# Splitting half of the feature weights on VectorE, and moving five smaller steps, in a hybrid decoder layer

## The chip, the core and the metric

The kernel runs on one core of a Trainium2 chip. The core has a matrix engine (TensorE, PE in the profile), three engines for element work (VectorE or DVE, ScalarE or ACT, GpSimd or POOL), a sync engine (SyncE or SP) that starts most transfers, and DMA engines that carry them. Each engine works through its own queue in order, and waits where an operand isn't there yet. The metric is the device time of one execution, in microseconds (us).

## What is computed

One decoder layer on 512 tokens of width 1024, everything in float32:

```python
proj = x @ w_in                                   # split into the ten inputs below
ret  = retention_chunkwise(rope(rq), rope(rk), rv)           # 4 heads x 128, chunks of 128
ret  = silu(rg) * (group_norm(ret) * ret_gn_gain)
sel  = indexer_topk(rope(iq), rope(ik), iw, topk=128)        # 8 heads x 64: top 128 keys a query
att  = sparse_attention(rope(aq), rope(ak), av, sel)         # 4 heads x 128
x = layer_norm(ALPHA * x + concat([ret, att]) @ w_out)
gate, up = split(x @ w_gate_up)                              # hidden width 2816
return layer_norm(ALPHA * x + (silu(gate) * up) @ w_down)
```

## The kernel before, in words

**Products of three.** A float32 operand is split into a high and a low part, and a product is three matmuls: high by high, high by low, low by high (`mm3`, L93 to L96). `split` (L85) makes the parts. ScalarE casts the high part (L86). The low part is source minus high part, and there are two ways to it. Kind "V": one subtraction on VectorE (L91). Kind "Q": ScalarE copies the negated high part (L88), and a DMA that POOL issues adds the source to it on its way (L89).

**The stream of weights.** `stream` (L172) lists the weight tiles of the projections and of the output projection with the kind of each of a tile's two halves. `wf` are the eight tiles of feature weights: keys and queries of attention, keys and queries of retention, so sixteen halves, k = 0 to 15. `weight` (L280) hands out a half and prepares three halves ahead: it puts `split` into the queues. The high and low parts live in four buffers each (`wh`, `wl`), the raw weights in three.

**The order.** The program's order is written by hand, with Python generators. The main generator yields at places between matmuls; at each of these, side generators are moved on. `pace(it, r)` moves a side generator by r units of its own cost figures a yield. `slots(main, plan)` runs the functions that `plan` lists for a yield's number. What is emitted first stands first in its engine's queue; the engines run at their own speed from there.

**The stages.**
- 0 to 28 us: the indexer's projection.
- 28 to 133 us: `proj_feature`, sixteen halves of 24 matmuls (`pf`). After each, VectorE turns the result by the rotary tables (`rope`, L217 to L219) and POOL adds (L221). Beside it runs `side`: `index_rope` (indexer's keys and queries: VectorE, POOL and POOL's DMAs), `logits` (scores, for query blocks 1 to 3: narrow matmuls `lg`, ScalarE, VectorE's sums), `topk` (48 rounds on VectorE, 16 for each block, over 256, 384 and 512 columns: a MAX8 at L388 and a replacement at L389).
- 133 to 217 us: `proj_token` for attention values, retention values and the gate (`pt`). Beside it, the rest of `side` and the 27 steps of `retention` (L517): scores, keys, states, outputs, then for each of the four chunks the norm (`ret_norm`, with a power on POOL, L426), `ret_scale` on VectorE (L502), `ret_gate` on POOL (L507) and `ret_turn`, which transposes the result on TensorE (L514, `rz`). At the end `att_score(0)`.
- 217 to 286 us: `mix_part`, the output projection, with attention in its slots: `sc_(b)` moves `att_score(b)` on by a step (scores and their maxima; exponentials; scaling by the sums, L550), `tr_` transposes (`apt`, L559), `pv_` multiplies by the values, `gate_(n)` splits the first gate weights.
- 286 to 308 us: the first gate blocks (`g_first`), between them the last norm (`sum_(3)`, `norm_half`, L620 and L621) and `combine` (L883), which forms sums and differences of token blocks for a product with fewer matmuls. `turn_` transposes such a tile (`trs`, L636), `rest` makes its low part (L642).
- 308 to 520 us: `g_cycle`, once for each of 22 hidden blocks. Each has gate and up weights, from which VectorE forms differences (`g_sum`, L762); `g_conv` splits the pieces A to D of the next blocks (`gh2C` and `gl2C` are the high and low part of block 2's piece C).
- 520 to 654 us: the down projection, the final norm, the stores.

Of the kernel before, what the change touches and what calls it, by code (L numbers as in the profile page):

```python
# [17 lines left out]
D = 1024  # L18
# [35 lines left out]
def hybrid_layer_kernel(ctx: ExitStack, tc: tile.TileContext, xT, x, pos, w0, wf, wt, wo,  # L54
# [114 lines left out]
        yield  # L169


    stream = [(wf[c], "VV" if c == 0 else "QQ") for c in range(8)]  # L172
    stream += [(wt[g, i], "QQ") for g in (1, 2, 0) for i in range(2)]
    stream += [(wo[c], "VV") for _ in range(2) for c in range(4)]
    limit = [len(stream)]
# [138 lines left out]
    def proj_feature(c):  # L314
        for i in range(2):
            h, l = weight()
            acc = psd(f"pf{c}_{i}")

            def items(acc=acc, h=h, l=l):
                for kt in range(KT):  # L320
                    cs = slice(kt * P, kt * P + P)
                    yield lambda cs=cs, kt=kt: mm3(acc, h[:, cs], l[:, cs], xh[kt], xl[kt], kt == 0, kt == KT - 1)

            yield from dense(list(items()), lambda i=i, acc=acc: rope(feats[c // 2][:, 2 * (c % 2) + i], acc, CT, ST), 3)
# [69 lines left out]
    def chain(*its):  # L394
        for it in its:
            yield from it

    def pace(it, r, credit=0.0):
        while True:
            credit += r  # L400
            while credit > 0.0:
                c = next(it, 0.0)
                credit -= 1.0 if c is None else c
                if c == 0.0:
                    break
            yield

    def run(main, *sides):
        for _ in main:
            for s in sides:  # L410
                next(s, None)
# [105 lines left out]
    def retention():  # L517
        steps = (((ret_keys, 0),), ((ret_score, 0),), ((ret_keys, 1),), ((ret_state, 0),), ((ret_score, 1),), ((ret_out, 0, 0),),
                 ((ret_out, 0, 1),), ((ret_state, 1),), ((ret_keys, 2), (ret_scale, 0)), ((ret_score, 2),), ((ret_out, 1, 0),),
                 ((ret_out, 1, 1),), ((ret_state, 2),), ((ret_score, 3), (ret_scale, 1)), ((ret_out, 2, 0), (ret_gate, 0)),  # L520
                 ((ret_out, 2, 1),), ((ret_gate, 1),), ((ret_out, 3, 0), (ret_scale, 2)), ((ret_out, 3, 1),), ((ret_turn, 0), (ret_gate, 2)),
                 ((ret_scale, 3),), ((ret_turn, 1), (ret_gate, 3)), (), ((ret_turn, 2),), (), ((ret_turn, 3),), ())
        for step in steps:
            for f, *a in step:
                f(*a)
            yield
# [52 lines left out]
    lg = chain(*[logits(j) for j in range(1, NB)])  # L579
    tk = chain(*[topk(j) for j in range(1, NB)])  # L580
    side = chain(index_rope(), lg, tk)
    run(chain(*[proj_feature(c) for c in range(4)]), pace(side, 1.0, -1.0))
    run(chain(*[proj_feature(c) for c in range(4, 8)]), pace(side, 1.0))
    run(proj_token(1), pace(side, 1.5))
    rt["decay"] = big.tile([P, 2, HEADS * P], F32, tag="s7", name="decay")
    dma(rt["decay"], decay_d)
    mixt[0] = unit("s8", "mrh", F32R), unit("s10", "mrl", F32R)
    rets = retention()
    run(proj_token(2), pace(side, 1.6), pace(rets, 1.2))
    tail = chain(rets, att_score(0))  # L590
    run(proj_token(0), pace(side, 1.2), pace(tail, 1.4))
    drain(tail)


# [85 lines left out]
    def slots(main, plan, *sides):  # L680
        for n, _ in enumerate(main):
            for f in plan.get(n, ()):
                f()
            for s in sides:
                next(s, None)

    def tr_(b, h):
        return lambda: att_tr(b, h)

    def pv_(b, h):  # L690
        return lambda: att_pv(b, h)
# [3 lines left out]
    def sc_(b):  # L695
        return lambda: next(sc[b])

    sums = {}

    def sum_(b):  # L700
        def f():
            sums[b] = norm_sum(x1[b], accm[b])
        return f
# [15 lines left out]
    def gate_(n):  # L719
        def f():  # L720
            hl = big.tile([P, 2, 1024], F32R, tag=("s6", "s7", "s9", "s1")[n], name=f"gb{n}")
            split(V, hl[:, 0], hl[:, 1], gates[n // 2][:, n % 2])
            gw[n, "B"] = hl[:, 0], hl[:, 1]
        return f
# [4 lines left out]
                           6: [sc_(1), pv_(0, 2)], 7: [pv_(0, 3)], 9: [tr_(1, 0)], 10: [tr_(1, 1)], 11: [tr_(1, 2), pv_(1, 0)],  # L729
                           12: [tr_(1, 3), pv_(1, 1)], 13: [pv_(1, 2)], 14: [pv_(1, 3), sc_(2)], 15: [gate_(0)]}, pace(side, 0.6))  # L730
    drain(side)
    slots(mix_part(0, 1), {0: [sc_(2)], 1: [gate_(1)], 2: [sc_(3)], 3: [sc_(2)], 5: [tr_(2, 0)], 6: [tr_(2, 1), sc_(3)], 7: [tr_(2, 2), pv_(2, 0)],
                           8: [tr_(2, 3), pv_(2, 1), sc_(3)], 9: [pv_(2, 2)], 10: [pv_(2, 3), gate_(2)], 11: [sum_(0)], 12: [tr_(3, 0), gate_(3)],
                           13: [tr_(3, 1)], 14: [tr_(3, 2), pv_(3, 0)], 15: [sum_(1), tr_(3, 3), pv_(3, 1)]})
    slots(mix_part(1, 0), {0: [pv_(3, 2), end_(0)], 1: [pv_(3, 3), end_(1)], 9: [early_(0, 0)], 10: [early_(0, 1)],
# [79 lines left out]
    def g_cycle(n, between=None):  # L815
        nxt = n + 1 if FIRST <= n + 1 < NF else None
        g_mm(n, "a", "A", 0, "s2", False)
        if n:
            g_end(n - 1)
        if between:  # L820
            next(between)
        gp[n]["c"] = psu(f"gc{n}")[:, :Q]
        g_mm(n, "c", "A", 1, "s1", True)
        t = tmp(f"gt{n}")
        gp[n]["t2"], gp[n]["t7"] = t[:, :Q], t[:, Q:]
        A.copy(gp[n]["t2"], gp[n]["a"])
        if n:
            g_conv(n + 1, "A")
        if nxt:
            g_open(nxt)  # L830
            g_mm(nxt, "a", "B", 0, "11", True)
        g_mm(n, "a", "C", 0, "s3", False)
        if nxt:
            g_t1(nxt)
            g_mm(nxt, "b", "B", 1, "12", True)
        c = gp[n]["c"]
        if n == NF - 1:
            c = tmp("gc")[:, :Q]
            A.copy(c, gp[n]["c"])
            g_mm(n, "c", "D", 0, "s4", False)  # L840
        A.copy(gp[n]["t7"], gp[n]["a"])
        V.tensor_tensor(gp[n]["t7"], gp[n]["t7"], c, op=ALU.add)
        if between:
            next(between)
        if n == 0:
            g_conv(1, "A")
        if n + 2 >= FIRST:
            g_conv(n + 2, "B")
        g_mm(n, "a", "C", 1, "22", False)
        if nxt:  # L850
            g_u1(nxt)
        g_sum(n + 2)
        g_conv(n + 1, "C", V if n > 1 else None)
        if n == 0:
            for m in range(FIRST):
                g_silu1(m)
        if n < NF - 1:
            g_mm(n, "c", "D", 0, "s4", False)
        A.activation(gp[n]["h2"], gp[n]["a"], AF.Silu)
        g_conv(n + 1, "D", V if n > 1 else None)  # L860
        g_load(n + 4)

    g_load(0)
# [24 lines left out]
    def g_first(n, which):  # L888
        g_mm(n, "ab"[which], "B", which, ("11", "12")[which], True)
        if which == 0:  # L890
            g_t1(n)
# [5 lines left out]
    g_first(0, 1)  # L897
    g_open(1)
    g_first(1, 0)
    sum_(3)()  # L900
    combine(2, G, ("s1", "s4"))
    g_add1(0)
    turn_("s2", 2)
    for i in range(2):
        norm_half(x1[3], *sums[3], gb, i)
    combine(3, V, ("s3", "s2"))
    g_first(1, 1)
    g_add1(1)
    combine(3, V, ("s1",))
    rest("s2", 2)  # L910
    g_open(2)
    g_first(2, 0)
    g_first(2, 1)
    g_open(3)
    g_first(3, 0)
    turn_("s2", 3)
    g_add1(2)
    rest("s2", 3)
    g_sum(1, V, slice(0, 2))
    g_first(3, 1)  # L920
    for b in (2, 3):
        turn_("s1", b)
        rest("s1", b)
# [249 lines left out]
```

## Time and profile before

| | |
|---|---|
| device time, median of 3 runs | 651.93 us (650.21 to 652.14) |
| profiled execution | 656.79 us |
| its span, first to last instruction | 654.0 us |
| TensorE busy | 626.8 us (96%) |
| VectorE busy | 473.7 us (72%) |
| ScalarE busy | 295.3 us (45%) |
| POOL busy | 118.8 us (18%) |

How to read it: the engines overlap, so their busy times don't add up. Where one engine is busy for nearly the whole span, the time is its work plus its waits. A busy share is a mean over stages; what a stage is limited by is read from its own windows. The granted clock is the share of its full speed that the chip gave TensorE in a stretch; a matmul's busy time grows when it falls.

### The profile page before, as it was taken

What the parts mean: (1) busy time and instruction counts of PE and PEld (TensorE: products, weight loads), DVE (VectorE), ACT (ScalarE), POOL (GpSimd) and SP (SyncE); (2) the same over time, 40 slices, a digit from 0 to 9 for tenths busy, and PEclk for the clock granted to TensorE, in tenths of its full rate; (3) what the DMA queues carried; (4) which work ended last, traced back from release to release, by engine and by line L of the source; (5) the groups of instructions that cost most, each with busy time, mean ns of one, the idle gap of its engine ahead of it and who ended that gap; (6) DMA issues with size and microseconds to landing.
All of it is one profiled execution on the core that took longest, in us unless ns stands there. A gap on an engine that the chain in (4) does not pass through costs nothing.

```text
span 654.0 us, 9798 instructions
## 1 busy us (share of the span) xinstructions
PE 626.8 (96%) x3792; PEld 558.0 (85%) x3792; DVE 473.7 (72%) x883; ACT 295.3 (45%) x514; POOL 118.8 (18%) x128
## 2 busy tenths in 40 slices
PE   9998899999999999998799999999999999999993
PEld 7976788888887868888699999999999988888883
DVE  6668378997879567999659888898898864333265
ACT  5625355334334657444645555555555643311100
POOL 1559623421373000041300000000000000000012
PEclk9999799999999999999989999999999999999997
DMA  8877975788543851352741332322313362321012
GB/s 301 276 215 176 210 201 138 169 197 213 136 122 121 306 218 65 128 129 69 162 142 67 127 116 79 129 81 114 130 65 129 129 208 82 129 99 62 2 43 86
DMA packets 25438, 91.14 MB, mean 139 GB/s; under 512 B 3056, under 2 KB 4208, under 8 KB 19760
## 3 DMA queue, kind: packets, MB, share of 16 engines
q1 hardware_dynamic: 18592, 71.51, 31.9%
q0 software_dynamic: 6224, 18.09, 14.3%
q10 hardware_dynamic: 576, 0.92, 0.4%
q8 instruction: 29, 0.48, 0.3%
q14 instruction: 17, 0.14, 0.1%
HBM read 69.80 MB, written 2.10 MB: 110 GB/s over the span
## 4 chain that ended last, share of the span: by engine, by line
PE 47%; DVE 6%; issue 2%; DMA 1%; POOL 1%; ACT 1%; DVEq 0%; POOLq 0%
PE ga L787 17%; PE gc L787 9%; PE gb L787 4%; PE dl L95 3%; PE dl L96 3%; PE dl L94 3%; PE dr L96 3%; PE dr L95 3%; PE dr L94 3%; DMA gl2C<-gs 1%; DVE gs L762 1%; DVE wl L91 1%; POOL rs L426 1%; DVE parts L642 1%; DVE cs L883 1%
## 5 line engine op out<-in xcount | busy, mean ns | idle before, releaser
L426 POOL TENSOR_TENSOR rs<-ve,half 128x1 f32<-128x1 f32 (+1 forms) x12 | 15.0, 1254 | 392.5 <-DVE ve L425 392.5
L86 ACT CAST wh<-raw 128x1024 fp32r<-128x1024 f32 x44 | 46.1, 1050 | 53.6 <-issue 20.1
L91 DVE TENSOR_TENSOR dl<-draw,dh 128x1024 fp32r<-128x1024 f32 x22 | 26.9, 1223 | 59.1 <-ACT dh L86 59.1
L96 PE MATMUL pf<-xh,wl 128*128 128x512 f32 x128 | 51.4, 402 | 4.9 <-DMA wl<-raw 4.9
L86 ACT CAST dh<-draw 128x1024 fp32r<-128x1024 f32 x22 | 23.2, 1053 | 69.5 <-PE dl L96 38.6
L94 PE MATMUL pf<-xh,wh 128*128 128x512 f32 x128 | 51.0, 398 | 0.0
L95 PE MATMUL pf<-xl,wh 128*128 128x512 f32 x128 | 50.9, 398 | 0.0
L94 PE MATMUL pt<-wh,xh 128*128 128x512 f32 x96 | 39.1, 407 | 0.0
L96 PE MATMUL pt<-wh,xl 128*128 128x512 f32 x96 | 37.5, 391 | 0.0
L95 PE MATMUL pt<-wl,xh 128*128 128x512 f32 x96 | 37.4, 390 | 0.0
L89 POOL DMA_DIRECT2D wl<-raw x26 | 23.7, 926 | 70.6 <-ACT wl L88 65.4
L96 PEld LDWEIGHTS pf<-xh,wl 128*128 128x128 f32 x128 | 24.7, 193 | 11.4 <-DMA wl<-raw 6.2
L94 PE MATMUL dl<-dh,h 128*128 128x512 f32 x88 | 34.2, 389 | 0.0
L95 PE MATMUL dl<-dl,h 128*128 128x512 f32 x88 | 34.2, 389 | 0.0
L96 PE MATMUL dl<-dh,h 128*128 128x512 f32 x88 | 34.2, 389 | 0.0
L96 PE MATMUL dr<-dh,h 128*128 128x512 f32 (+1 forms) x88 | 33.4, 379 | 0.0
L95 PE MATMUL dr<-dl,h 128*128 128x512 f32 (+1 forms) x88 | 33.4, 379 | 0.0
L94 PE MATMUL dr<-dh,h 128*128 128x512 f32 (+1 forms) x88 | 33.4, 379 | 0.0
L762 DVE TENSOR_TENSOR gs<-graw,gs 128x512 f32<-128x512 f32 x44 | 30.3, 688 | 0.8
L762 DVE TENSOR_TENSOR gs<-graw 128x512 f32<-128x512 f32 x44 | 30.1, 684 | 0.0
L91 DVE TENSOR_TENSOR wl<-raw,wh 128x1024 fp32r<-128x1024 f32 x18 | 21.8, 1220 | 9.9 <-ACT wh L86 9.9
L95 PEld LDWEIGHTS pf<-xl,wh 128*128 128x128 f32 x128 | 24.7, 193 | 4.9
(960 smaller groups left out, 1948.8 us busy)
## 6 DMA issues: line engine op xcount, KB each, us to landing
graw<-in_wgu_dram SPq DMA_DIRECT2D x22, 1024.0 KB, 4.8
wl<-raw POOLq DMA_DIRECT2D x26, 512.0 KB, 5.8
draw<-in_wd_dram SPq DMA_DIRECT2D x22, 512.0 KB, 4.6
raw<-in_wf_dram SPq DMA_DIRECT2D x8, 1024.0 KB, 8.5
raw<-in_wo_dram SPq DMA_DIRECT2D x8, 1024.0 KB, 5.0
raw<-in_wt_dram SPq DMA_DIRECT2D x6, 1024.0 KB, 6.1
w0s<-in_w_dram SPq DMA_DIRECT2D x8, 320.0 KB, 5.0
x<-in_x_dram SPq DMA_DIRECT2D x4, 512.0 KB, 5.0
```

Source lines behind the costliest of these rows:

```text
L86: A.copy(hi, src)
L89: nc.gpsimd.dma_start(lo.bitcast(F32), src, accum_op=ALU.add)
L91: eng_lo.tensor_tensor(lo, src, hi.bitcast(F32), op=ALU.subtract)
L94: T.matmul(acc, lhsT=lh, rhs=rh, start=first, stop=False, **kw)
L95: T.matmul(acc, lhsT=lh, rhs=rl, start=False, stop=False, **kw)
L96: T.matmul(acc, lhsT=ll, rhs=rh, start=False, stop=last, **kw)
L426: G.tensor_tensor(r[:, :n], e[:, :n], half[:, :n], op=ALU.pow)
L642: V.tensor_tensor(lo, turned[q, b], hi.bitcast(F32), op=ALU.subtract)
L762: eng.tensor_tensor(t[dst], a, b, op=ALU.subtract)
L787: T.matmul(gp[n][acc], lhsT=a[:, i * S + k * P:i * S + k * P + P], rhs=parts[q][:, b, k], start=first and j == 0, stop=j == 11, skip_group ...
L883: engs.tensor_tensor(c[q], how[q][0], how[q][1], op=how[q][2])
```

## The change

Five edits, all to order and place; what is computed stays the same.

1. In `stream`, the even half of each of the feature tiles 1 to 7 becomes kind "V"; the odd halves stay "Q". Tile 0 was "VV" and stays so. The side work's paces change: lower in the feature chunks, higher in the token projections.
2. In `retention`'s steps, `ret_gate(2)` moves ahead of `ret_out(3, 1)`, whose last act is the last norm.
3. In the slots of `mix_part(0, 1)`, the third step of `att_score(2)` (its scaling) moves from slot 3 to slot 2, and block 3's scores and `gate_(1)` move behind it, to slot 3.
4. Among the first gate blocks, `combine(2, G, …)` on POOL moves ahead of `sum_(3)`; one half of the last norm, `combine(3, …)` and two `g_first` move.
5. In `g_cycle`, block 1's piece C is split right behind the first copy to `gt` (L826) of cycle 0, and pieces C and D of block 2 become kind "V" where they were "Q".

```diff
-    stream = [(wf[c], "VV" if c == 0 else "QQ") for c in range(8)]
+    stream = [(wf[c], "VV" if c == 0 else "VQ") for c in range(8)]
...
-                 ((ret_out, 2, 1),), ((ret_gate, 1),), ((ret_out, 3, 0), (ret_scale, 2)), ((ret_out, 3, 1),), ((ret_turn, 0), (ret_gate, 2)),
+                 ((ret_out, 2, 1),), ((ret_gate, 1),), ((ret_out, 3, 0), (ret_scale, 2)), ((ret_gate, 2), (ret_out, 3, 1)), ((ret_turn, 0),),
...
-    run(chain(*[proj_feature(c) for c in range(4)]), pace(side, 1.0, -1.0))
-    run(chain(*[proj_feature(c) for c in range(4, 8)]), pace(side, 1.0))
-    run(proj_token(1), pace(side, 1.5))
+    run(chain(*[proj_feature(c) for c in range(4)]), pace(side, 0.85, -1.0))
+    run(chain(*[proj_feature(c) for c in range(4, 8)]), pace(side, 0.85))
+    run(proj_token(1), pace(side, 1.7))
...
-    run(proj_token(2), pace(side, 1.6), pace(rets, 1.2))
+    run(proj_token(2), pace(side, 1.8), pace(rets, 1.2))
...
-    run(proj_token(0), pace(side, 1.2), pace(tail, 1.4))
+    run(proj_token(0), pace(side, 1.5), pace(tail, 1.4))
...
-    slots(mix_part(0, 1), {0: [sc_(2)], 1: [gate_(1)], 2: [sc_(3)], 3: [sc_(2)], 5: [tr_(2, 0)], 6: [tr_(2, 1), sc_(3)], 7: [tr_(2, 2), pv_(2, 0)],
+    slots(mix_part(0, 1), {0: [sc_(2)], 2: [sc_(2)], 3: [sc_(3), gate_(1)], 5: [tr_(2, 0)], 6: [tr_(2, 1), sc_(3)], 7: [tr_(2, 2), pv_(2, 0)],
...
         A.copy(gp[n]["t2"], gp[n]["a"])
         if n:
             g_conv(n + 1, "A")
+        else:
+            g_conv(1, "C", None)
...
-        g_conv(n + 1, "C", V if n > 1 else None)
+        if n:
+            g_conv(n + 1, "C")
...
-        g_conv(n + 1, "D", V if n > 1 else None)
+        g_conv(n + 1, "D", V if n else None)
...
+    combine(2, G, ("s1", "s4"))
     sum_(3)()
-    combine(2, G, ("s1", "s4"))
     g_add1(0)
     turn_("s2", 2)
-    for i in range(2):
-        norm_half(x1[3], *sums[3], gb, i)
-    combine(3, V, ("s3", "s2"))
+    norm_half(x1[3], *sums[3], gb, 0)
     g_first(1, 1)
     g_add1(1)
-    combine(3, V, ("s1",))
+    norm_half(x1[3], *sums[3], gb, 1)
+    combine(3, V, ("s3", "s2"))
     rest("s2", 2)
     g_open(2)
     g_first(2, 0)
     g_first(2, 1)
+    combine(3, V, ("s1",))
     g_open(3)
     g_first(3, 0)
+    g_first(3, 1)
     turn_("s2", 3)
     g_add1(2)
     rest("s2", 3)
     g_sum(1, V, slice(0, 2))
-    g_first(3, 1)
```

What this does to the queues, at three places. First POOL's queue early in the feature chunks, in before: `wl4` and `wl5` are the low parts of the fifth and sixth half (k = 4 and 5), `kk3` the indexer's keys, `akT`, `qs` and `ql` results of ropes.

```order
L244 DMA kk3_359<-kk3_359 32x512
L89 DMA wl4_439<-raw2_279 128x1024
L221 TENSOR_TENSOR akT_362<-rt1_447,rt2_448 128x512
L250 TENSOR_TENSOR qs_465<-rt1_459,rt2_460 128x384
L251 TENSOR_TENSOR ql_358<-qs_465,qa_356 128x384
L89 DMA wl5_485<-raw2_279 128x1024
```

The same place in after:

```order
L244 DMA kk3_359<-kk3_359 32x512
L221 TENSOR_TENSOR akT_362<-rt1_445,rt2_446 128x512
L250 TENSOR_TENSOR qs_472<-rt1_466,rt2_467 128x384
L251 TENSOR_TENSOR ql_358<-qs_472,qa_356 128x384
L89 DMA wl5_483<-raw2_279 128x1024
```

The DMA for `wl4` is gone (VectorE makes it, ahead of the first rope of a chunk's result); the one for `wl5` stands where it stood, one DMA fewer behind the keys.

Second, VectorE's queue at the end of retention, in before: L425 is the last norm's variance, L437 the low part of a turned chunk, L502 `ret_scale(3)`, L388 and L389 one round of top-k.

```order
L425 TENSOR_SCALAR ve_1795<-mv_1786 128x4
L437 TENSOR_TENSOR mrl_1393<-rz0_1799,mrh_1392 128x4x128
L91 TENSOR_TENSOR wl28_1811<-raw14_1469,wh28_1810 128x1024
L502 TENSOR_SCALAR rz_1820<-ri3_1762,mv_1786,rs_1796 128x128 x4
L388 MAX m8_1837<-score_367 128x8
L389 MATCH_REPLACE score_367<-m8_1837,score_367 128x512
L437 TENSOR_TENSOR mrl_1393<-rz1_1840,mrh_1392 128x4x128
```

And in after:

```order
L425 TENSOR_SCALAR ve_1781<-mv_1772 128x4
L437 TENSOR_TENSOR mrl_1371<-rz0_1785,mrh_1370 128x4x128
L91 TENSOR_TENSOR wl28_1795<-raw14_1449,wh28_1794 128x1024
L388 MAX m8_1804<-score_367 128x8
L389 MATCH_REPLACE score_367<-m8_1804,score_367 128x512
L502 TENSOR_SCALAR rz_1807<-ri3_1746,mv_1772,rs_1782 128x128 x4
L388 MAX m8_1824<-score_367 128x8
L389 MATCH_REPLACE score_367<-m8_1824,score_367 128x512
L437 TENSOR_TENSOR mrl_1371<-rz1_1827,mrh_1370 128x4x128
```

A round of top-k over 512 columns stands ahead of the last scaling, where none stood between the same rows.

Third, VectorE's queue in cycle 1 of the gate blocks, in before: `gs3` are differences for block 3, L811 to L813 the closing sums of block 0.

```order
L762 TENSOR_TENSOR gs3_2_2975<-graw3_2769 128x512
L762 TENSOR_TENSOR gs3_3_2976<-graw3_2769,gs3_1_2974 128x512
L811 TENSOR_TENSOR gt1_2939<-gt1_2939,gc1_2926 128x256
L812 TENSOR_TENSOR hu0_2583<-hu0_2583,gt1_2939 128x256
L813 TENSOR_TENSOR hu0_2583<-hu0_2583,gt1_2939 128x256
```

And in after:

```order
L762 TENSOR_TENSOR gs3_2_2968<-graw3_2762 128x512
L762 TENSOR_TENSOR gs3_3_2969<-graw3_2762,gs3_1_2967 128x512
L91 TENSOR_TENSOR gl2C_2975<-gs2_2_2874,gh2C_2974 128x512
L91 TENSOR_TENSOR gl2C_2975<-gs2_3_2875,gh2C_2974 128x512
L91 TENSOR_TENSOR gl2D_2994<-graw2_2564,gh2D_2993 128x512
L811 TENSOR_TENSOR gt1_2932<-gt1_2932,gc1_2919 128x256
L812 TENSOR_TENSOR hu0_2576<-hu0_2576,gt1_2932 128x256
L813 TENSOR_TENSOR hu0_2576<-hu0_2576,gt1_2932 128x256
```

Three subtractions (the two halves of `gl2C`, and `gl2D`) now stand between the differences and the closing sums; the ScalarE copies and POOL DMAs that made them before are gone.

## Rows read from the trace of the kernel before

**Rows 1.** page, totals: busy us (share of the span), number of instructions.

```profile
PE 626.8 (96%) x3792; PEld 558.0 (85%) x3792; DVE 473.7 (72%) x883; ACT 295.3 (45%) x514; POOL 118.8 (18%) x128
```

**Rows 2.** waits of PE: instruction <- releaser: us in total, times, longest.

```profile
PE pf L96 <- DMA wl<-raw: 4.9, 3, 2.7
...
PE ga L787 <- DMA gl2C<-gs: 3.6, 1, 3.6
...
PE trs L636 <- DVE cs L883: 1.5, 1, 1.5
...
PE apt L559 <- DVE ast L550: 1.4, 1, 1.4
...
PE rz L514 <- POOL rzz L507: 1.1, 1, 1.1
```

**Rows 3.** windows: us, PE PEld DVE ACT POOL busy, PEclk, DMA share, GB/s.

```profile
50.00:60.00 10.00, 8.95 (x40) 7.04 (x39) 9.76 (x16) 5.56 (x8) 9.54 (x12) 1.00 0.68 129
...
60.00:70.00 10.00, 7.27 (x28) 5.65 (x27) 3.53 (x6) 3.77 (x5) 9.84 (x14) 0.82 0.96 224
...
290.00:300.00 10.00, 8.49 (x73) 8.29 (x72) 9.71 (x16) 2.29 (x5) 3.78 (x3) 1.00 0.00 0
...
320.00:330.00 10.00, 6.29 (x41) 5.79 (x40) 2.84 (x6) 2.23 (x6) 1.49 (x2) 0.79 0.77 176
```

**Rows 4.** timeline of PE, feature chunks: start, us, instruction, xcount [idle <-releaser].

```profile
52.80 0.50 PE L96 MATMUL pf<-xh,wl 128*128 128x512 f32 x1 [1.05 <-DMA wl<-raw]
...
63.95 0.39 PE L95 MATMUL pf<-xl,wh 128*128 128x512 f32 x1
...
67.07 0.79 PE L96 MATMUL pf<-xh,wl 128*128 128x512 f32 x1 [2.73 <-DMA wl<-raw]
...
73.21 0.44 PE L94 MATMUL pf<-xh,wh 128*128 128x512 f32 x1
```

**Rows 5.** timeline of POOL, feature chunks: issues of accumulating DMAs.

```profile
47.93 0.96 POOL L89 DMA_DIRECT2D wl<-raw  x1
...
52.55 0.87 POOL L89 DMA_DIRECT2D wl<-raw  x1
...
61.23 0.90 POOL L89 DMA_DIRECT2D wl<-raw  x1
```

**Rows 6.** timeline of DVE, feature chunks: one operation, twice.

```profile
49.26 1.40 DVE L248 TENSOR_TENSOR qa<-rt,rt 128x384 fp32r<-128x384 f32 x1
...
56.79 0.56 DVE L248 TENSOR_TENSOR qa<-rt,rt 128x384 fp32r<-128x384 f32 x1
```

**Rows 7.** groups of DVE by shape: busy us, mean ns | idle before.

```profile
L91 DVE TENSOR_TENSOR wl<-raw,wh 128x1024 fp32r<-128x1024 f32 x18 | 21.8, 1220 | 9.9 <-ACT wh L86 9.9
...
L388 DVE MAX8 m<-score 128x8 f32<-128x384 f32 x16 | 9.0, 560 | 0.5
```

**Rows 8.** timeline of DVE, POOL and PE, from retention to the attention scores.

```profile
160.55 0.69 DVE L456 TENSOR_TENSOR rst<-rs,decay 128x512 f32<-128x512 f32 x1 [3.48 <-DMA decay<-in_decay_dram]
...
203.67 1.30 POOL L507 TENSOR_TENSOR rzz<-rz,grg 128x512 f32<-128x512 f32 x1 [0.33 <-DVE rz L502]
...
208.03 0.60 PE L514 MATMUL rz<-ident,rzz 128*128 128x128 f32 x4
...
216.45 1.89 PE L538 MATMUL as<-akT,aqT 128*128 128x256 f32 x8
```

**Rows 9.** timeline of PE, gate pieces C and D of blocks 1 and 2.

```profile
315.28 0.38 PE L787 MATMUL ga<-parts,gh1C 128*128 128x256 f32 x1 [0.90 <-ACT gt L826]
...
318.97 0.28 PE L787 MATMUL gc<-parts,gh1D 128*128 128x256 f32 x1
...
327.20 0.58 PE L787 MATMUL ga<-parts,gl2C 128*128 128x256 f32 x1 [3.63 <-DMA gl2C<-gs]
...
332.95 0.28 PE L787 MATMUL gc<-parts,gh2D 128*128 128x256 f32 x1
```

## The prediction

> **What bounds the kernel now.** I read the page's totals first: TensorE is busy 626.8 us of the span of 654.0, VectorE 473.7, ScalarE 295.3 [rows 1]. So only two things can change the end by much: TensorE's idle time, and stretches in which its matmuls run at the lower clock. Second, TensorE's waits by releaser [rows 2]: nearly all of it lies in five places, and the change touches each. Third, the windows [rows 3]: the granted clock is 0.82 in the stretch with the longest wait of the feature chunks and 0.79 in the one with the longest of all, and 1.00 in the one ahead of them. A wait there costs more than its own length, because matmuls behind it run at 1.2 instead of 2.4 GHz for a while. Fourth, the timelines, for when each late thing would have been due.
>
> **Feature chunks (the kinds in `stream`).** Sixteen halves, k = 0 to 15, of 24 matmuls; between waits they start every 0.228 us (52.80 to 63.95, 49 steps) [rows 4]. The waits fall on k = 2, 4 and 6, each on a low half that a POOL-queued accumulating DMA delivers: 4.9 us idle, the longest 2.7 [rows 2]. After that one, 13 chunk matmuls and two narrower ones for the indexer scores take 6.14 us, 67.07 to 73.21 [rows 4]; at the pitch above, 13 × 0.228 and some 0.2 for the narrow ones, they would take about 3.2, so 2.9 is lost beyond the idle time. The loss is 4.9 + 2.9 = 7.8.
>
> All three late halves are even ones, and VectorE now makes the low parts of the even ones. Seven subtractions of 1.22 [rows 7], 8.5 us, join VectorE's queue; seven DMA issues of about 0.9 [rows 5] leave POOL's, and seven negated copies ScalarE's. Even halves no longer wait for a DMA. The odd ones do, and POOL's queue decides. For k = 5 the issue was at 52.55, and one issue of 0.96 less stands ahead of it, so 51.6. From issue to use it was 47.93 to 52.80, 4.87, and 61.23 to 67.07, 5.84 [rows 4, 5]. With 4.87 the low part of k = 5 is there at 56.5. It is due 24 steps after 52.80, at 58.3, less the 2.2 us of the two waits that are gone: 56.1. That is 0.4 late. But VectorE's subtraction now falls between POOL's tensor operations. The same VectorE operation took 1.40 at 49.26 and 0.56 at 56.79 [rows 6]: beside a busy POOL an operation with two input streams is stretched, and I take it that POOL's are too. If one such meeting costs POOL 1.2, about one subtraction, the issue is at 52.8 and k = 5 is 1.6 late. I take this end, since POOL has no gap there: 9.54 of 10 us busy [rows 3]. For k = 7 the same chain, with 4.87 to 5.84 from issue to use, gives 0.2 to 1.1 late, 0.8 taken; from k = 8 on the old order had no wait. So 2.4 of the 7.8 stays: gain **5.4**, bounds 3 (k = 5 lowers the clock as the 2.73 did) and 7.8 (no wait).
>
> The Trainium skill (SBUF — State Buffer, "Who interferes with whom") says that a VectorE instruction with two SBUF inputs contends with a GpSimd instruction that reads SBUF. This rule speaks against moving these splits to VectorE: by it k = 5 is 1.6 late and the sum below 12.9; without it 0.4 and 14.1. The two rows of 1.40 and 0.56 agree with it.
>
> Nothing stands behind the copies that leave ScalarE: it is idle over half of the span. SyncE's loads keep their order and their three buffers.
>
> **Later top-k (the paces).** The side work's lower pace in the chunks (0.85 for 1.0) leaves VectorE room for the splits and puts top-k rounds into the token projections. By the order, 26 of 48 rounds instead of 31 stand ahead of retention's first keys, and all 48 still end ahead of attention block 0's scores, as before. So five rounds more stand between these points, each a MAX8 of 0.56 [rows 7], a replacement over the same 384 columns, taken as long, and a short load: about 1.2, 6.0 in all. VectorE's wait of 3.48 for the decay table [rows 8] takes up part; 2.5 stays, of which I take 1.7 at the last norm. One more round, 512 wide, now stands ahead of the last scaling: 1.46, an estimate, 0.56 × 512/384 twice.
>
> **Retention gate.** Gate 2 goes ahead of the last norm's power on POOL, which waits for VectorE. TensorE's wait of 1.1 for it [rows 2] goes: gain 1.3 with its slow restart. But gate 3 ended at 203.67 + 1.30 = 204.97 [rows 8]; plus 1.7 and 1.46 that is 208.1. Turn 3 started at 208.03 [rows 8], is now due at 206.7, and so waits 1.4. Attention block 1's scores (216.45) [rows 8] need PSUM tiles that block 0's reductions on VectorE free, and VectorE is up to the whole 6.0 late there; I count 1.5 lost over scores and transposes. Gate and later top-k together: 1.3 − 1.4 − 1.5, about **−1.5**, a loss. Bounds +1.3 (the slack swallows the rounds) and −4 (the scores wait 4.0 instead of 1.5).
>
> **Softmax scaling.** Block 2's scaling goes one slot earlier, ahead of block 3's scores and the gate split. TensorE's wait of 1.4 before the transposes [rows 2] goes; VectorE has the same pieces in another order, and the moved ones aren't needed until block 3's transposes nine slots on. Gain **1.4**, bounds 0 (the lag above reaches this far) and 1.4.
>
> **Block sums.** POOL's two sums go ahead of VectorE's `sum_(3)`, and a gate group fills the pause before block 3's turn. TensorE's wait of 1.5 [rows 2] goes there, but VectorE is full at this point, 9.71 of 10 us in 290 to 300 [rows 3], and the next block's matmuls still need the rests that it makes. What TensorE doesn't wait before, it mostly waits after. Gain **0.5**, bounds 0 and 1.5.
>
> **Gate C and D splits.** C(1)'s split starts earlier, so that ScalarE's queue is free for the next copy of `gt`: the 0.90 that TensorE waits at 315.28 [rows 9] goes, gain **0.9**. C(2)'s low parts no longer go through ScalarE, POOL and a DMA. They landed so late that TensorE was idle 3.63 at 327.20, and the group then took 5.75 (to 332.95), where C(1)'s took 3.69 (315.28 to 318.97) [rows 9]: a loss of 3.6 + 2.1 = 5.7. On VectorE the three low halves of C(2) and D(2) take some 0.7 each (half the columns of 1.22 [rows 7], with an estimated 0.1 for the start), and it was busy only 2.84 of 10 us in 320 to 330 [rows 3]. They follow C(2)'s casts and the next block's differences and end at about 320.7 by its queue; they are due at about 322.3, a margin of 1.6. Gain **5.7**, bounds 4 (the margin is gone) and 5.7.
>
> **The sum.** 5.4 − 1.5 + 1.4 + 0.5 + 0.9 + 5.7 = 12.4, and 0.5 for the smaller waits on the same copies: **12.9 us**. The profiled execution took 656.79 for its span of 654.0, 4.9 above the median of 651.93. The same cut puts its like at 643.9, its span at 641.1 and the median at **639.0**. The bounds together make +3.9 and +19.1.
>
> **Rivals.**
> A. The chunks' waits only change place: odd halves are late in place of even ones, and the clock falls with them. For it: POOL keeps the odd halves' DMAs and is full to 60, and one wait of 2.73 was enough for the clock. Against it: half as many DMAs. The 5.4 shrinks to 0, 7.5 is gained: **644.4**. That the change doesn't do what it says (even halves still late, now on their casts) comes out here as well.
> B. No lag: the later rounds are swallowed, k = 5 lands in time, every term is at its upper bound. For it: VectorE is busy only 3.53 of 10 us in 60 to 70 [rows 3]. Against it: the slack of 3.48 is less than the 6.0 that is added. 19.1 is gained: **632.8**.
> C. Slower: VectorE's in-order queue becomes the bound of the chunks. The subtractions stand behind ropes and score sums, and TensorE has a lead of three halves, 3 × 24 × 0.228 = 16 us. Once VectorE's lag exceeds that, k = 6 to 14, five halves, are late; at the cost of the worst so far, 2.7 + 2.9, that is 28, less the 7.8 of the old waits and the 7.5 of the other edits: 12.7 slower, **664.6**. For it: VectorE is 9.76 of 10 us busy in 50 to 60 [rows 3]. Against it: 3.53 in the next ten, room for what is added.
>
> **How the numbers follow.** The forecast has a chance of 0.70, A 0.15, B 0.09, C 0.04; 0.02 lies between A and C, within 0.3% of before, about what a measurement of this kernel can tell from no change. The forecast's own bounds are 635 to 644; the range goes on to B at 632 and past A, to 646. Faster by over 0.3%: 0.94 (forecast, A, B); within: 0.02; slower: 0.04.
>
> **What will show it.** Right: no wait on an even half, at most about 3 us on odd ones up to 75 us, no clock under 0.9 there; no wait on `gl2C`, and a clock of 1.00 around 325; none on block 2's `ast`; a new one of about 1.4 on retention's last turn, or at the scores behind it. Wrong: `pf` waits of 5 us or more with a low clock (A), waits on VectorE's `wl` in the chunks (C), or waits on VectorE of over 4 us between 205 and 250, by which the later rounds would cost more than I gave them.

## The result, and the profile after

The changed kernel takes 647.35 us (median of 6 runs, 646.18 to 648.33) against 652.03 for the kernel before, timed beside it: a ratio of 0.9932, interval 0.9913 to 0.9951. That is 4.7 us less by the medians, where 12.9 were forecast, and above 646, the upper end of the range. The profiled execution took 646.18, its span is 643.7; of before they were 656.79 and 654.0. The trace of after is the shortest of its six executions (spans 643.7 to 645.9, granted clock 0.994 in the trace and 0.987 to 0.990 in the others), so a median execution of after has more low clock than the trace shows. One execution of 2196 us, of the version with the last pace at 1.0, is left out of its median and its ratio.

The page's totals of after, in the columns of [rows 1]:

```profile
PE 623.4 (97%) x3792; PEld 555.0 (86%) x3792; DVE 485.2 (75%) x893; ACT 287.5 (45%) x504; POOL 110.6 (17%) x118
```

VectorE has 11.5 us more, ScalarE 7.8 and POOL 8.2 less, as the edits say; TensorE's is 3.4 shorter with the same number of matmuls: the granted clock over the span is 0.994, where it was 0.984. The waits of TensorE in after, in the form of [rows 2]:

```profile
PE as L538 <- DVE mrl L437: 4.2, 1, 4.2
...
PE lg L369 <- DVE score L375: 1.4, 1, 1.4
...
PE rz L514 <- POOL rzz L507: 0.7, 1, 0.7
...
PE ga L787 <- ACT gt L843: 0.9, 2, 0.5
...
PE pf L96 <- DMA wl<-raw: 0.2, 1, 0.2
```

All five waits of [rows 2] are gone or small: on the DMA of a low half 4.9 became 0.2, and those on `gl2C`, `cs` and `ast` don't appear. Two new ones have come, both on VectorE: 4.2 on attention block 0's scores (`as`), 1.4 on the indexer's scores (`lg`). The 0.9 on `gt` is not new: before waits as long on the same copy, there in L841. The windows of after, in the columns of [rows 3]:

```profile
60.00:70.00 10.00, 9.81 (x45) 7.80 (x44) 8.34 (x10) 5.69 (x9) 6.95 (x8) 1.00 0.57 131
...
200.00:210.00 10.00, 5.08 (x26) 3.87 (x25) 9.79 (x22) 1.63 (x2) 1.28 (x1) 0.95 0.30 108
...
210.00:220.00 10.00, 10.00 (x41) 8.16 (x41) 7.00 (x28) 5.90 (x14) 0.00 (x0) 0.88 0.49 187
...
320.00:330.00 10.00, 9.54 (x79) 9.34 (x78) 9.00 (x18) 5.56 (x12) 0.00 (x0) 1.00 0.32 115
```

The clock is at 1.00 in 60 to 70 (0.82 in [rows 3]) and in 320 to 330 (0.79). It is below it now from 200 to 220, around the new wait: 0.95 and 0.88.

This table gives TensorE's way through the program, from the start of the first matmul of one kind to the first of the next. Since the profiled execution of before was 4.8 us above its median, the same kernel was profiled once more (`before_again`, below), and both stand here.

| from, to | before | before again | after | after less before | after less before again | forecast |
|---|---|---|---|---|---|---|
| start to `pf` | 27.90 | 28.51 | 27.76 | −0.14 | −0.75 | 0 |
| `pf` to `pt` (chunks) | 104.71 | 100.78 | 99.54 | −5.2 | −1.2 | −5.4 |
| `pt` to `rz` (projections, retention) | 63.08 | 63.08 | 63.03 | 0.0 | 0.0 | 0 |
| `rz` to `mx` (turns, scores) | 22.30 | 22.60 | 27.83 | +5.5 | +5.2 | +1.5 |
| `mx` to `ga` (output projection) | 67.91 | 67.87 | 66.36 | −1.6 | −1.5 | −1.4 |
| `ga` to `gc` (first gate blocks) | 18.11 | 18.14 | 17.40 | −0.7 | −0.7 | −0.5 |
| `gc` to block 3's `gc` (C and D splits) | 31.80 | 30.03 | 24.60 | −7.2 | −5.4 | −6.6 |
| from there to the end | 318.14 | 318.13 | 317.19 | −1.0 | −0.9 | 0 |
| span | 653.95 | 649.14 | 643.71 | −10.2 | −5.4 | |

Against the trace that the prediction was made from, the chunks gave 5.2 of the 5.4 forecast, and the only row far off is that from the turns to `mx`. Against the second trace of the same kernel the chunks gave 1.2. The experiments settle both rows. The 0.9 in the last row lies behind TensorE's last matmul, in the final norm and the stores, which no edit touches: from block 3's `gc` to that matmul all three traces take 307.4. Its cause stays open.

The place of the new wait, in the timeline of VectorE, ScalarE and TensorE in after:

```profile
184.18 0.69 DVE L475 TENSOR_TENSOR rstate<-rstate,rkv 128x512 f32<-128x512 f32 x1 [3.30 <-POOL rstate L474]
...
202.86 0.59 ACT L436 CAST mrh<-rz 128x512 fp32r<-128x512 f32 x1 [3.96 <-PE rz L514]
...
204.04 1.14 PE L538 MATMUL as<-akT,aqT 128*128 128x128 f32 x6
...
205.69 0.69 DVE L388 MAX8 m<-score 128x8 f32<-128x512 f32 x1
...
207.20 0.69 DVE L388 MAX8 m<-score 128x8 f32<-128x512 f32 x1
...
208.60 0.68 DVE L437 TENSOR_TENSOR mrl<-rz,mrh 128x512 fp32r<-128x512 f32 x1
...
209.33 0.80 PE L538 MATMUL as<-akT,aqT 128*128 128x128 f32 x2 [4.15 <-DVE mrl L437]
```

Three of block 0's four heads had a free PSUM tile at 204.04. The fourth needs the tile that retention's last turn (`rz`) holds until VectorE has made its low part (L437). Its high part is there at 202.86 + 0.59 = 203.45, but the subtraction stands behind top-k rounds in VectorE's queue, starts at 208.60, and TensorE goes on at 209.33, 4.15 late. From 204.04 to the first `mx` at 218.16 it is 14.1 us; before took 8.1 for the same: 4.15 of idle time, the rest at the lower clock of the two windows.

The same place in before:

```profile
188.42 0.69 DVE L475 TENSOR_TENSOR rstate<-rstate,rkv 128x512 f32<-128x512 f32 x1 [3.29 <-POOL rstate L474]
...
209.86 1.28 PE L538 MATMUL as<-akT,aqT 128*128 128x128 f32 x8
...
209.92 0.68 DVE L437 TENSOR_TENSOR mrl<-rz,mrh 128x512 fp32r<-128x512 f32 x1
```

The lines of the two kernels also tell which of the later rounds count. L475, a sum in retention's states, is the last place where VectorE sits idle ahead of that subtraction, 3.29 us in before and 3.30 in after. From there to the subtraction VectorE's queue has 7 rounds and takes 21.5 us in before, 9 rounds and 24.4 us in after. So two of the later rounds, 2.9 us, are on the way; the others stand ahead of a gap that VectorE has in both kernels. Counted from the first `pt`, the subtraction starts 4.0 us later than in before: 2.9 by the two rounds, 1.1 because L475 comes later. TensorE reaches the scores 0.5 earlier.

### The profile page after: what moved, and what is told of

Same layout as the page of the kernel before. It is cut to its first block, busy times and chain, and to the rows that moved or that the text cites. A ratio compares the mean times of both kernels' runs of the same rounds, so it can differ in the third digit from the quotient of the medians.

```text
span 643.7 us, 9760 instructions
## 1 busy us (share of the span) xinstructions
PE 623.4 (97%) x3792; PEld 555.0 (86%) x3792; DVE 485.2 (75%) x893; ACT 287.5 (45%) x504; POOL 110.6 (17%) x118
## 4 chain that ended last, share of the span: by engine, by line
PE 53%; DVE 4%; POOL 0%; issue 0%; ACT 0%; DVEq 0%; POOLq 0%
PE ga L787 19%; PE gc L787 10%; PE gb L787 5%; PE dl L95 3%; PE dl L96 3%; PE dl L94 3%; PE dr L96 3%; PE dr L95 3%; PE dr L94 3%; DVE wl L91 1%; DVE part L642 0%; POOL rs L426 0%; PE mx L95 0%; DVE gs L762 0%; PE mx L96 0%
## 5 line engine op out<-in xcount | busy, mean ns | idle before, releaser
L96 PE MATMUL pf<-xh,wl 128*128 128x512 f32 x128 | 50.1, 391 | 0.3 <-DMA wl<-raw 0.2
L91 DVE TENSOR_TENSOR wl<-raw,wh 128x1024 fp32r<-128x1024 f32 x25 | 32.5, 1308 | 14.8 <-ACT wh L86 14.8
L94 PEld LDWEIGHTS pf<-xh,wh 128*128 128x128 f32 x128 | 24.0, 188 | 4.5
```

The source lines that it names most:

```text
L91: eng_lo.tensor_tensor(lo, src, hi.bitcast(F32), op=ALU.subtract)
L94: T.matmul(acc, lhsT=lh, rhs=rh, start=first, stop=False, **kw)
L96: T.matmul(acc, lhsT=ll, rhs=rh, start=False, stop=last, **kw)
```

## Experiments

Each time stands as a ratio to the kernel before, which ran on the same chip beside it.

**The kernel before, once more.** No edit.

> The kernel before, unchanged, profiled a second time. Its first profiled execution took 656.79 us, 4.8 above the median of its timed runs. Theory 1 (the waits of that trace are in every run, and the 4.8 lie around the span): the span is again about 654, with waits on the low halves of 4.9 us, on gl2C of 3.6, and windows at a granted clock of 0.8 after both. Theory 2 (that execution had one stretch at the low clock that most have not): a span of about 649 to 650, with one of the two stretches (60 to 80 us, or 320 to 340) at a clock near 1.0; its idle time is then still there, but shorter by the matmuls that run at half rate behind it.

Median 652.77, ratio 1.0003 (0.998 to 1.0027); span of the profiled execution 649.1. Its waits, and its windows:

```profile
PE pf L96 <- DMA wl<-raw: 4.1, 2, 3.0
...
PE ga L787 <- DMA gl2C<-gs: 2.8, 1, 2.8
```

```profile
60.00:70.00 10.00, 6.96 (x32) 5.45 (x31) 3.59 (x6) 3.58 (x6) 9.92 (x13) 1.00 0.95 222
...
70.00:80.00 10.00, 10.00 (x53) 8.61 (x52) 6.38 (x13) 4.59 (x10) 5.56 (x5) 1.00 0.98 235
...
320.00:330.00 10.00, 6.76 (x44) 6.26 (x43) 5.47 (x10) 3.45 (x8) 0.00 (x0) 0.83 0.81 204
```

The wait on the low halves is there, and the longest, 3.0, is longer than the 2.7 of [rows 2]. But the clock stays at 1.00 behind it, where the first trace had 0.82 in 60 to 70. So the 2.9 us of half-rate matmuls that I counted among the chunks' loss don't belong to every execution. The spans and granted clocks of 63 runs of before say how often it may have been so: from 648.3 at 0.990 to 654.4 at 0.984, median 650.7; nine of them have a granted clock as low as 0.984 or 0.985, and one alone is longer than the 653.95 of the execution that I read. Theory 2 holds. The low clock around `gl2C`, 0.83, is in both traces, if shorter here.

**The C and D splits alone.**

```diff
+        else:
+            g_conv(1, "C", None)
...
-        g_conv(n + 1, "C", V if n > 1 else None)
+        if n:
+            g_conv(n + 1, "C")
...
-        g_conv(n + 1, "D", V if n > 1 else None)
+        g_conv(n + 1, "D", V if n else None)
```

> The kernel before with the fifth edit alone (splits of gate pieces C and D). Theory 1: every run of before has the 3.6 us wait on gl2C and the low clock behind it, so this edit alone takes 6.6 to 7.2 us off the median, to about 645. Theory 2: the low clock there is not in every run, and 4 to 5 us come off. A rival, that the wait only moves to the next block's pieces: 0 to 2 us off.

Median 646.28, ratio 0.9909 (0.9878 to 0.9939): 5.9 us by the ratio, 6.5 by the medians. By the ratios this one edit brings more than the whole change does, though the two intervals overlap.

```profile
320.00:330.00 10.00, 9.54 (x79) 9.34 (x79) 8.62 (x16) 5.34 (x11) 0.00 (x0) 1.00 0.36 134
```

The clock is 1.00, and `gl2C` is not waited for. The forecast of 6.6 for this edit is right, within what the interval allows (4.0 to 8.0 us); the time lies between the two theories of the expectation.

**The even halves on VectorE alone, with the paces of before.**

```diff
-    stream = [(wf[c], "VV" if c == 0 else "QQ") for c in range(8)]
+    stream = [(wf[c], "VV" if c == 0 else "VQ") for c in range(8)]
```

> The kernel before with the even halves of the feature chunks split on VectorE and nothing else, the paces as before. Theory 1: the waits on the low halves and the low clock behind the third go, 5 us less, if the side work does not need the lower pace; without it, waits on VectorE of 1 to 3 us turn up in the chunks, and 3 to 4 come off. Theory 2: the low clock behind the third wait is not in every run of before, and 2 to 3 us come off the median. Retention and attention have the queue order of before, so no wait of several us at the scores.

Median 652.87, ratio 1.0001 (0.9983 to 1.0018): nothing gained, a miss of both theories.

```profile
PE lg L369 <- DVE score L375: 4.6, 1, 4.6
```

```profile
70.00:80.00 10.00, 7.56 (x25) 6.29 (x26) 8.43 (x14) 2.05 (x4) 4.52 (x4) 0.66 0.65 173
```

The chunks' waits on DMAs are gone and one of 4.6 has come: the indexer's score matmuls need a PSUM tile that VectorE empties (L375), and VectorE is behind its splits and ropes. The clock is 0.66 in the ten us around it. One of the added splits, in VectorE's and POOL's timeline, shows how VectorE falls behind:

```profile
65.04 1.61 POOL L221 TENSOR_TENSOR akT<-rt,rt 128x512 f32<-128x512 f32 x1
...
65.08 2.66 DVE L91 TENSOR_TENSOR wl<-raw,wh 128x1024 fp32r<-128x1024 f32 x1 [1.42 <-ACT wh L86]
```

Ahead of the split VectorE sat idle for 1.42, until ScalarE had cast the high part, with ropes and score sums standing behind the split in its queue. The split then took 2.66, where the group's mean in before was 1.22 [rows 7]; a POOL operation that reads two tiles started 0.04 ahead of it. This is rival C's mechanism, VectorE's queue as the bound of the chunks, at a smaller price than I gave it and at another place: the indexer's scores, not the halves.

**The first edit whole: halves and paces.** The edit above and the five changed paces.

> The kernel before with the first edit whole: halves on VectorE and the changed paces. If the later top-k rounds cost what the trace of after shows between the last retention turn and the output projection (6.0 us), this is slower than halves_alone by about 6 us, and about as long as before (within 2 us). If that wait comes from the moved retention gate instead, it is as fast as halves_alone or faster, and shows no wait of 4 us at the scores.

Median 653.88, ratio 1.0017 (0.9999 to 1.0035): no faster than before, and not told apart from it or from the halves alone. So the expectation held against before, and not against the halves alone, which had gained nothing either.

```profile
PE rz L514 <- POOL rzz L507: 3.6, 1, 3.6
...
PE as L538 <- DVE mrl L437: 1.4, 1, 1.4
...
PE lg L369 <- DVE score L375: 1.4, 1, 1.4
```

The lower pace does what it is for: 1.4 on `lg` instead of 4.6, and the stretch from `pf` to `pt` takes 99.5 us as in after, against 103.5 with the halves alone. But the rounds that it moved come back on retention: 3.6 on the last norm's gate, 1.4 at the scores. Here the retention gate stands where it stood, and the price, 22.30 grown to 27.65 from `rz` to `mx`, is that of after. So the moved gate is not what makes the price; it decides whether TensorE pays it on the gate or at the scores.

**After without the first edit.** Halves and paces as in before, edits 2 to 5 kept.

> After without the first edit: the sixteen halves and the paces as in before, the other four edits kept. Theory 1 (the first edit as a whole costs time, because VectorE falls behind): the chunks wait for DMAs as in before (4 us idle), the scores do not wait, and the time is that of the fifth edit alone, 646.3, less what edits 2 to 4 bring in the trace (about 1.1, 1.4 and 0.6): 643 to 644, faster than after by 3 to 4 us. Theory 2 (edits 2 to 4 bring nothing, the first edit is neutral): 646 to 647, the same as after.

Median 643.03, ratio 0.9868 (0.984 to 0.9896), against 0.9932 for after: faster by 0.0064, 4.2 us, and the intervals don't overlap. Theory 1 holds.

```profile
PE pf L96 <- DMA wl<-raw: 3.6, 2, 2.5
...
PE as L538 <- DVE mrl L437: 1.3, 1, 1.3
```

The chunks wait for DMAs as before (their clock is 1.00 here too), and the scores wait 1.3. Edits 2 to 4 are the difference from the C and D splits alone, 0.0041, 2.7 us, with intervals that overlap; their terms in the forecast were 1.3, 1.4 and 0.5. By the two traces edit 3 brings 1.6 (`mx` to `ga`), edit 4 0.7 (`ga` to `gc`), and edit 2 nothing: from `rz` to `mx` it is 22.3 against 22.4, with 1.3 idle at the scores in place of 1.2 on the gate.

**After with the old paces,** the halves kept.

> After with the paces of before, the halves on VectorE kept. Theory 1 (the lag comes with the later rounds): no wait over 1 us between the last turn and the output projection; but a wait of some 4.6 us of the indexer's score matmuls on VectorE in the chunks with the low clock behind it, as in the halves alone; in all 643 to 645. Theory 2 (the moved retention gate makes the wait of 4.2 at the scores): it is still there, and the time is 647 or more.

Median 645.58, ratio 0.9900 (0.9873 to 0.9927), 2.1 us faster than after by the ratio, with intervals that overlap.

```profile
PE lg L369 <- DVE score L375: 4.5, 1, 4.5
...
PE as L538 <- DVE mrl L437: 1.4, 1, 1.4
```

The wait at the scores shrinks from 4.2 to 1.4 and the one in the chunks grows from 1.4 to 4.5. The rounds add to VectorE's queue in one place or the other; the paces choose where TensorE meets it. The 1.4 is not the later rounds': it is there with the halves and the paces of before too, where edit 2 is kept (1.3, above).

**After with the last pace at 1.0.** Rounds of top-k move behind block 0's scores: four by the expectation, three by the trace, where 45 of 48 stand ahead of them.

```diff
-    run(proj_token(0), pace(side, 1.5), pace(tail, 1.4))
+    run(proj_token(0), pace(side, 1.0), pace(tail, 1.4))
```

> After with one number changed: the side work's pace in the last token projection is 1.0 instead of 1.5, so that four rounds of top-k move from ahead of attention block 0's scores to behind them. Theory 1 (VectorE's queue at the last turned chunk is the wait): the 4.2 us at the scores shrink by two to four rounds of 1.46 each, to under 2, the low clock behind them goes, and 3 to 6 us come off: 641.5 to 644.5. Rival (the rounds are work that VectorE has to do before the softmax of block 2 anyway, so the wait only moves there): the waits turn up before 245 us on the scores of block 1 or the transposes, and the time stays within 1.5 us of after.

Median 641.27, ratio 0.9839 (0.9808 to 0.9869): 6.1 us faster than after by the ratio.

```profile
PE as L538 <- DVE mrl L437: 1.5, 1, 1.5
...
PE rz L514 <- POOL rzz L507: 0.8, 1, 0.8
```

The wait at the scores is 1.5 instead of 4.2, the clock from 200 to 220 is 1.00, and no wait turns up at the transposes of block 2. The rounds were not needed there yet; they only stood in the way.

**After with 1.15 in the last four feature tiles.** The rounds go earlier, into a stretch in which VectorE had gaps.

```diff
-    run(chain(*[proj_feature(c) for c in range(4, 8)]), pace(side, 0.85))
+    run(chain(*[proj_feature(c) for c in range(4, 8)]), pace(side, 1.15))
```

> After with one number changed in the other direction: the pace in the last four feature tiles is 1.15 instead of 0.85, so that top-k rounds move into the stretch from 90 to 130 us, where VectorE was idle for 8 us of 40; all rounds but none of the splits then stand ahead of the last two turns. Theory 1: the wait at the scores goes (4.2 and about 1.8 of low clock), the chunks gain no wait of over 1 us: 641 to 643. Rival: the indexer's score matmuls then wait for VectorE in the chunks, as with the old paces (4.6 us), and the time is 645 or more.

Median 641.71, ratio 0.9845 (0.9817 to 0.9874): 5.7 us faster than after.

```profile
PE rz L514 <- POOL rzz L507: 1.1, 1, 1.1
...
PE lg L369 <- DVE score L375: 1.4, 1, 1.4
```

```profile
200.00:210.00 10.00, 8.86 (x46) 7.19 (x45) 8.07 (x22) 4.38 (x11) 1.29 (x1) 1.00 0.38 138
```

No wait on `as` is left; VectorE is busy 8.07 of 10 us from 200 to 210, against 9.79 in after. From L475 to the last turn's low part VectorE now has 5 rounds and takes 19.3 us; with the last pace at 1.0 it has 6 and takes 20.3. Moving the rounds later or earlier gives the same 6 us back: so much was the price of VectorE's queue at that one place.

**The moved retention gate, undone in two surroundings:** in after, and in the version above.

```diff
-                 ((ret_gate, 2), (ret_out, 3, 1)), ((ret_turn, 0),),
+                 ((ret_out, 3, 1),), ((ret_turn, 0), (ret_gate, 2)),
```

> After with the second edit undone: gate 2 of retention is again behind the last norm on POOL. Theory 1 (VectorE's lag is what TensorE waits for, wherever it waits): the wait only sits one place earlier, some 3 to 4 us on the third turn (rz) on POOL's rzz and 1 to 2 at the scores, and the time is that of after within 1 us, 646.5 to 648.5. Theory 2 (the moved gate is worth its 1.1 us beside the lag): 1 to 1.5 us slower than after, 648.5 or more.

> The version with the pace of 1.15 in the last four feature tiles (641.7), and in it the second edit undone. There VectorE is not late, so this prices the moved gate by itself: if it is worth what TensorE's wait in before was (1.1 idle, 1.3 with its restart), this is 1 to 1.5 us slower, 642.8 to 643.3; if the wait only moves to the next thing that comes late (the gate or norm of the last block), the two are the same within 0.5 us.

In after, undoing it gives 645.30, ratio 0.9891 (0.9871 to 0.9911): 2.7 us faster than with it by the ratios, though the spans of the two traces are 643.3 and 643.7. That of after is the shortest of its executions; by the median spans it is 643.4 against 645.0. In the version with early rounds, undoing it gives 644.91, ratio 0.9877 (0.9853 to 0.99), against 0.9845: about 2.1 slower, with intervals that overlap. TensorE's waits in the first, then in the second:

```profile
PE rz L514 <- POOL rzz L507: 2.5, 1, 2.5
...
PE as L538 <- DVE mrl L437: 1.3, 1, 1.3
```

```profile
PE rz L514 <- POOL rzz L507: 2.6, 1, 2.6
```

```profile
200.00:210.00 10.00, 8.70 (x38) 7.20 (x39) 6.34 (x16) 2.57 (x4) 2.56 (x2) 0.83 0.36 122
```

With VectorE late, the wait is 2.5 and 1.3 in two places without the move and 0.7 and 4.2 with it: the move gathers it in one, where it is 1.1 longer in all. From `rz` to `mx` that is 26.5 us without the move and 27.8 with it, so 1.3 of the 2.7 is in the traces. That the timed runs are faster without it was expected by neither theory, and the cause of the rest stays open. With VectorE in time, the gate's wait is 2.6 without the move, the clock is 0.83 behind it, and the way from `rz` to `mx` takes 25.16 instead of 22.06. So the same edit is worth about 2 to 3 us there, costs 1 to 3 where VectorE lags, and by the traces brings nothing with the halves and paces of before.

**Both paces changed: 0.75 in the first four tiles, 1.2 in the last four.**

> After with two paces changed, 0.75 in the first four feature tiles and 1.2 in the last four: the indexer's score matmuls come later in the chunks, top-k rounds earlier than in after. If the 1.4 us wait of the score matmuls on VectorE and the 4.2 at the attention scores are both VectorE's lag, both go and this is the fastest version, 640 to 641.5. If the later score sums push the top-k rounds together, the wait at the attention scores stays in part and the time is 642 to 644.

Median 640.92, ratio 0.9817 (0.9796 to 0.9838): the fastest version, 7.5 us below after by the ratio, and faster than after without the first edit by 3.3.

```profile
PE rz L514 <- POOL rzz L507: 1.2, 1, 1.2
...
PE lg L369 <- DVE score L375: 1.1, 1, 1.1
...
PE pf L96 <- DMA wl<-raw: 0.6, 1, 0.6
```

No wait of TensorE is over 1.2 us, and the clock is at 1.00 in the chunks and at the scores. The 1.4 on `lg` has only become 1.1. So with such paces the first edit gains 3.3 us where with its own it cost 4.2. How much of that is the halves and how much the paces is not shown: the halves of before with these paces were not run.

## Why the prediction was wrong

**The direction and the small terms held.** Softmax scaling: 1.4 forecast, 1.5 to 1.6 by the table. Block sums: 0.5 and 0.7. C and D splits: 6.6 (0.9 + 5.7) forecast; 5.4 to 7.2 by the two traces, 5.9 timed alone. The margin of `gl2C` was forecast at 1.6; in after its two subtractions end at 317.04 + 1.29 = 318.33 and the first matmul that reads it starts at 320.16, so 1.8:

```profile
317.04 1.29 DVE L91 TENSOR_TENSOR gl2C<-gs,gh2C 128x512 fp32r<-128x512 f32 x2
...
320.16 0.28 PE L787 MATMUL ga<-parts,gl2C 128*128 128x256 f32 x1
```

**The term of the later top-k rounds was mis-sized:** −1.5 with the gate, −4 at its bound; measured −5.2 to −5.5 from `rz` to `mx`, and 5.7 to 6.1 by the two experiments that move the rounds away. The mechanism was named: VectorE up to 6 us late at block 0. The step that failed is the one after it, "I count 1.5 lost over scores and transposes". I took it that block 0's reductions are what TensorE waits for next, and that only block 1 needs the tiles they free. The trace of after shows a wait one step sooner, by the fourth head of block 0, for the tile that the last turn holds until L437. The whole lag at that instruction is on the path, 4.15 of it as idle time, and the matmuls behind run at the lower clock, which I had priced for the old waits and not for the new one. The gate's 1.3 was no gain of its own: with VectorE late, it moved the wait on.

The rounds themselves were counted at the wrong place. I set five of them, 6.0 us, against the 3.48 of the decay table. In after VectorE still sits idle for 2.29 at that instruction (155.12), and for 3.30 at 184.18: what stands ahead of these costs nothing, and the two rounds behind them have no slack at all. A 512-wide round, by the way, is 1.49 by my own formula and not 1.46; in after one takes 1.51, from 205.69 to 207.20.

**The term of the chunks was right for the trace and wrong for the median:** 5.4 forecast, 5.2 between the two traces, 1.2 against the second trace of before. The two other traces with the chunks of before, those of the C and D splits alone and of after without the first edit, have 101.1 and 100.3 there, so 1.6 and 0.8 over after. The step that failed is "the same cut puts … the median at 639.0". The execution that I read lay 4.9 above the median, and I carried all its losses over to a median run. 3.9 of the difference between the two traces of before is in the chunks, 1.8 at the C splits: the clock fell there in that execution more than in the other. The right use of the 4.9 was as a bound: a wait with a low clock behind it, in an execution slower than the median, may be counted twice over.

That 5.2 came so near to 5.4 was luck besides. Of the 7.8 I left 2.4 to the odd halves, 1.6 on k = 5 and 0.8 on k = 7; in after they wait 0.1 and 0.2. The meeting with VectorE for which I charged POOL 1.2 didn't hold up that DMA: it is issued at 51.09, where I had 52.8. VectorE paid instead, with 2.32 and 2.31 for the splits at 40.23 and 53.09, and TensorE's 1.4 on `lg`, which the forecast doesn't have, took the place of the 2.4.

The range, too, was narrower than its own terms: their bounds reach down to a gain of 3.9, a median of 648.0, which has room for 647.35; the upper end was put at 646 all the same.

**The rivals.** A did not happen: odd halves waited 0.3 in all. The forecast there, "at most about 3 us on odd ones", held. C was right in its mechanism, VectorE's in-order queue: it shows with the old paces as the 4.6 us on `lg`, with the new ones on retention and the scores. It was wrong in price, since TensorE meets the lag at one or two places and not at five halves, so that it ate the first edit's gain and left most of the others'. I had tied it to a lead of 16 us for the halves, when other products of VectorE, the indexer's scores and the turned chunk's low part, leave TensorE a lead of a few tiles of PSUM only.

## What to carry to other kernels

When work is moved onto an engine with gaps, follow its queue to each place where another engine waits for a buffer that it frees, not only for data that it makes; the shortest lead among them sets the price. Count the rounds that stand between the queue's last idle time and that place, and put them ahead of the gap: here two numbers in a pace took 7.5 us off, where the split with its first paces had gained nothing. And before a loss at a low clock is summed, see whether the profiled execution is as long as the median; if it isn't, the surplus is likely in that loss.

## What was not expected of the hardware

**VectorE beside POOL.** `qa` (L248), 0.56 alone and 1.40 in [rows 6], took 2.97 in after, from 63.48, with two POOL operations that read SBUF in its time (the 0.56 at 56.79 in before had none beside it: POOL's last one ended at 56.81):

```profile
63.48 2.97 DVE L248 TENSOR_TENSOR qa<-rt,rt 128x384 fp32r<-128x384 f32 x1
...
63.45 1.61 POOL L221 TENSOR_TENSOR akT<-rt,rt 128x512 f32<-128x512 f32 x1
...
64.71 1.32 POOL L250 TENSOR_TENSOR qs<-rt,rt 128x384 f32<-128x384 f32 x1
```

The three end one after the other: POOL's first at 65.06, its second at 66.03, `qa` at 66.45. The Trainium skill (SBUF — State Buffer, "Who interferes with whom") says of VectorE's two-port modes that whoever issues first gets the shared pair for the whole instruction and the other fully blocks; for an instruction with two SBUF inputs it says that it contends with a GpSimd instruction that reads SBUF. The trace agrees that they contend, and shows how far it goes: beside two such POOL operations in a row, VectorE's took over five times as long.

**The clock.** In four traces the longest DMA wait in the chunks is 2.5 to 3.0 us with the same work around it (before twice, the C and D splits alone, after without the first edit): the clock fell in one of the four, 0.82, and was 1.00 in three. A wait of 2.6 on `rz` brought 0.83 in another place. Six traces have the same wait of 1.4 on `lg` near 77: in after the clock from 70 to 90 stays at 1.00, with the last pace at 1.0 it is 0.93 and 0.90 in the two windows. What decides it was not found; the length of the wait alone does not.
